# RWKV scan on the array's diagonal: 64x64x64 products in a parity-major layout, with ranks for its steps

## The chip, the cores and the metric

The kernel runs on one core of one Trainium2 chip. The metric is the device time of one execution in microseconds (us). The program is one launch; its engines are TensorE (PE; its weight loads are listed as PEld), VectorE (DVE), ScalarE (ACT), GpSimd (POOL) and SyncE (SP), and the DMA engines work from queues that an engine feeds. The trace's names with a q behind (SPq, ACTq) are what an engine's sequencer does itself, such as issuing a DMA.

## What is computed

One block of a diffusion transformer on 1024 tokens and 256 context tokens, width 1024, all in float32. The token mixer runs neighbourhood attention and a bidirectional RWKV-7 scan side by side, gates and merges them; an expert-choice mixture of experts follows.

```python
def rwkv_scan(r, decay, k, a, v, kk, S0, reverse, emit):
    def step(S, inp):
        r_t, w_t, k_t, a_t, v_t, kk_t = inp
        sa = jnp.einsum('bhvk,bhk->bhv', S, -kk_t)
        S = (S * w_t[:, :, None, :] + sa[..., None] * (kk_t * a_t)[:, :, None, :]
             + v_t[..., None] * k_t[:, :, None, :])
        y = jnp.einsum('bhvk,bhk->bhv', S, r_t) if emit else None
        return S, y
...
    for d in range(2):
        S_ctx, y_c = rwkv_scan(rc, *dirs_c[d], vrc, kkc, S0, d == 1, emit_ctx)
        _, y_l = rwkv_scan(r, *dirs[d], vr, kk, S_ctx, d == 1, True)
...
    y_rw = rwkv_readout(ys[0] + ys[1], r, v, [dirs[0][1], dirs[1][1]], g, p)
    out = (gate_na * (y_na @ p['w_pa']) + gate_rw * (y_rw @ p['w_pr'])) @ p['w_o']
```

There are 8 heads of 64 in the scan and 8 in the attention. `emit_ctx` is False here: the context is scanned only for its last state.

## The kernel before

**Stages.** Modulation and layer norms come first (to about 75 us). Then, to about 880 us, `proj` multiplies the tokens with slices of `w_in` (L258; each slice is loaded by SP's queue, split by ScalarE and GpSimd into a high and a low part, and multiplied in three passes), and for each of four pairs of heads `ct` and each direction `d` the function `feat` works out what the scan needs. It cuts the 1280 tokens into 20 chunks of 64 and takes them in five groups of four (`jb`), 40 groups in all. A group makes X (the scaled keys and receptances), BK (its partner), the masked products AQ of both, and BT (BK transposed on TensorE); SP's queue stores them to device memory as XD (L419), AQD (L430, L432), aD (L435) and BTD (L441). `inv` and `inv_off` make the 64x64 inverses of each chunk, WD; the last part of an inverse, `inv_off`, runs two passes of 32x32 products (L319), each copied by ScalarE (L320), and stores the result (L323).

**The scan** (`rwkv_chain`, L514 to L570) runs 20 step pairs, four over the context and sixteen "main" ones; a pair is one chunk in each direction, and the directions do not depend on each other. A step loads X, AQ, BT, its inverse WT (two DMAs, L533) and V (into the lower half of UV, L534), then
- L538: X times the state S, four products of 128x128 into RY; S holds each head's 64x64 on the diagonal of a 128x128 block, its other parts are zero;
- L541: the masked products times UV, added to RY; GpSimd has cleared the unused halves of AQ and UV (L529);
- L545, L546: R is minus the upper half of RY, the even heads copied by ScalarE, the odd ones by DVE;
- L550: the inverse times R, eight products of 64x64 that lie by turns in the upper left and the lower right quarter of the array;
- L553: the result copied to UV, half by DVE and half by ScalarE;
- L556: BT times UV, eight products; L561 and L562: DVE adds them to S and scales S by the decay, once for each half of the partitions;
- main steps only, L565 and L568: the masked products times UV once more, for the output Y, which ScalarE copies and whose store it issues from its own queue.

**What runs beside it.** After the features of the last pair 7 of the 16 slices of gates are left (`on_gate`, the same L258). Attention (`attention`, L572 to L660) runs 32 blocks, eight for each pair of heads. A block has score products (L588 to L591), maxima and scalings on DVE (L592 to L599), an exponential on ScalarE, and transposes and products with V (L606, L613). For each new pair of heads it loads K and Q in pieces (`qz`), rotates them on GpSimd and splits them on ScalarE and DVE. `readout` (L662) turns the outputs of the scan into the branch's features, `branch` (L699) multiplies either branch with its output weights, and `merge_top` and the experts follow.

**The order** is the framework's: it walks the program once and gives each engine its list of instructions, by priority; the priority is the place in the program, and `low_priority(tc,n)` puts what is in it n places back. The scan stands in the program ahead of the remaining gates and attention. A tile has one or two buffers; the queue of an engine is executed strictly in its order.

## Time and profile before

| | us |
|---|---|
| median of 3 runs | 3224.84 (3218.99 to 3229.81) |
| profiled execution, its own time | 3227.2 |
| span of its trace | 3225.4 |
| mean granted TensorE clock (share of full speed) | 0.953 |

Times below are us from the start of the span. In the tables by stretch "busy (x)" is the engine's busy time and its number of instructions, PEclk the clock that TensorE was granted, as a share of full speed, and DMA share the mean busy share of the 16 DMA engines. In the timeline a row is a run of alike instructions: its start, its length from the first start to the last end, and how many. An fp32 product leaves two records, each with its weight load.

### The profile page before, as it was taken

To read this page: it belongs to the slowest core of one execution; us is meant where nothing else is said; L and a number is where in the kernel's file an instruction comes from. 1 tells how busy PE (TensorE), PEld (TensorE's weight loads), DVE (VectorE), ACT (ScalarE), POOL (GpSimd) and SP (SyncE) were. 2 spreads that over 40 slices of the span, in tenths; PEclk is the share of its full clock that TensorE was granted. 3 is DMA by queue.
4 is the path that set the end of the run, shared out by engine and by line. 5 is a ranking of instruction groups with operands and counts; after the bars stand their busy time and mean duration, and the time that the engine had idled before them with its cause. 6 is when DMAs were issued, how large, how long until landed. Compare 5 with 4: busy or idle time off the path is not lost.

```text
span 3225.4 us, 47429 instructions
## 1 busy us (share of the span) xinstructions
PE 2975.9 (92%) x17900; PEld 2366.1 (73%) x17900; DVE 2361.4 (73%) x3207; ACT 1742.2 (54%) x2006; POOL 639.5 (20%) x511
## 2 busy tenths in 40 slices
PE   7999999997878978899879999999999999999995
PEld 4777776776667764477668888888888878888884
DVE  5245455544376769757788999888898888888887
ACT  5343343433234334322357777777777777777775
POOL 2233333333241227211000000111010111010004
PEclk8998999998889999899889999999999999999998
DMA  5245554555778766444589999999999999999985
GB/s 205 82 121 137 124 128 123 129 142 131 158 185 203 189 166 219 146 152 151 198 315 384 388 372 370 357 363 377 380 362 363 358 365 376 381 362 362 363 319 229
DMA packets 537641, 825.18 MB, mean 256 GB/s; under 512 B 206590, under 2 KB 335742, under 8 KB 537284
## 3 DMA queue, kind: packets, MB, share of 16 engines
q1 hardware_dynamic: 490876, 747.60, 67.5%
q10 hardware_dynamic: 41176, 55.01, 5.4%
q0 software_dynamic: 5360, 19.54, 2.3%
q8 instruction: 141, 2.31, 0.3%
q14 instruction: 88, 0.72, 0.1%
HBM read 732.49 MB, written 89.55 MB: 255 GB/s over the span
## 4 chain that ended last, share of the span: by engine, by line
PE 45%; DVE 8%; issue 4%; DMA 3%; ACT 2%; POOL 1%; ACTq 0%; POOLq 0%; DVEq 0%; SPq 0%
PE ph L1016 22%; PE ye L1031 14%; DVE lo L915 4%; PE po L752 3%; PE pA L709 2%; PE pt L1053 1%; DMA raw<-in_w_e_dram 1%; ACT hi L914 1%; DVE oh L856 0%; DVE dl L1055 0%; PE pl L828 0%; PE apt L606 0%; PE yp L613 0%; DVE s L599 0%; DMA wmod<-in_w_mod_dram 0%
## 5 line engine op out<-in xcount | busy, mean ns | idle before, releaser
L915 DVE TENSOR_TENSOR lo<-raw,hi 128x2048 fp32r<-128x2048 f32 (+1 forms) x560 | 1197.5, 2170 | 107.9 <-ACT hi L914 92.0
L914 ACT CAST hi<-raw 128x2048 fp32r<-128x2048 f32 (+1 forms) x560 | 1009.8, 1813 | 353.7 <-PE ph L1016 191.0
L1016 PE MATMUL ph<-lo,xh 128*128 128x512 f32 (+1 forms) x1536 | 456.7, 378 | 23.4 <-DVE lo L915 23.1
L1016 PE MATMUL ph<-hi,xh 128*128 128x512 f32 (+1 forms) x1536 | 448.9, 374 | 3.1 <-ACT xh L886 2.0
L1016 PE MATMUL ph<-hi,xl 128*128 128x512 f32 (+1 forms) x1536 | 448.2, 373 | 0.0
L1016 PEld LDWEIGHTS ph<-lo,xh 128*128 128x128 f32 x1536 | 267.6, 188 | 95.4 <-DVE lo L915 48.3
L1016 PEld LDWEIGHTS ph<-hi,xh 128*128 128x128 f32 x1536 | 271.5, 188 | 55.9 <-ACT xh L886 2.4
L1016 PEld LDWEIGHTS ph<-hi,xl 128*128 128x128 f32 x1536 | 270.8, 188 | 52.7
L258 PE MATMUL pp<-uh,whi 128*128 128x512 f32 (+1 forms) x832 | 266.2, 392 | 4.8 <-DVE th L334 3.1
L258 PE MATMUL pp<-ul,whi 128*128 128x512 f32 (+1 forms) x832 | 267.4, 392 | 0.0
L258 PE MATMUL pp<-uh,wlo 128*128 128x512 f32 (+1 forms) x832 | 261.8, 387 | 0.5 <-issue 0.3
L864 POOL DMA_INDIRECT gath<-table,idx x16 | 37.9, 2368 | 958.6 <-DVE oh L856 587.7
L1031 PE MATMUL ye<-lo,dh 128*128 128x512 f32 x704 | 222.5, 397 | 1.1 <-DVE lo L915 0.9
L1031 PE MATMUL ye<-hi,dh 128*128 128x512 f32 x704 | 219.7, 393 | 2.5 <-ACT hi L914 1.3
L1031 PE MATMUL ye<-hi,dl 128*128 128x512 f32 x704 | 218.9, 392 | 3.3 <-DVE dl L1055 3.3
L258 PEld LDWEIGHTS pp<-uh,whi 128*128 128x128 f32 x832 | 155.0, 195 | 42.2 <-issue 7.1
L258 PEld LDWEIGHTS pp<-uh,wlo 128*128 128x128 f32 x832 | 156.6, 196 | 38.2 <-issue 8.8
L258 PEld LDWEIGHTS pp<-ul,whi 128*128 128x128 f32 x832 | 156.3, 196 | 37.5 <-issue 10.0
L292 DVE TENSOR_TENSOR tmp<-AU,W 120x144 f32<-120x144 f32 (+24 forms) x248 | 93.0, 375 | 115.8 <-DMA WD<-AU 40.0
L1031 PEld LDWEIGHTS ye<-hi,dl 128*128 128x128 f32 x704 | 132.8, 189 | 32.1 <-DVE dl L1055 3.7
L207 POOL TENSOR_TENSOR wlo<-wraw,whi 128x512 fp32r<-128x512 f32 x86 | 113.6, 1341 | 211.4 <-ACT whi L206 141.0
L1031 PEld LDWEIGHTS ye<-hi,dh 128*128 128x128 f32 x704 | 131.1, 189 | 30.7 <-ACT hi L914 2.0
(334 smaller groups left out, 4488.8 us busy)
## 6 DMA issues: line engine op xcount, KB each, us to landing
raw<-in_w_e_dram SPq DMA_DIRECT2D x430, 1024.0 KB
raw<-in_w_e_dram SPq DMA_DIRECT2D x128, 768.0 KB
wraw<-in_w_in_dram SPq DMA_DIRECT2D x86, 256.0 KB
wmod<-in_w_mod_dram SPq DMA_DIRECT2D x48, 256.0 KB
BTD<-BT SPq DMA_DIRECT2D x40, 256.0 KB
cBT<-BTD SPq DMA_DIRECT2D x40, 256.0 KB
wmod<-in_w_mod_dram SPq DMA_DIRECT2D x16, 512.0 KB
XD<-X SPq DMA_DIRECT2D x32, 256.0 KB
```

The costliest lines, as they stand in the source:

```text
L207: nc.gpsimd.tensor_sub(l[:,ks],r,h[:,ks].bitcast(F32))
L258: nc.tensor.matmul(p,wt[:,k,:],ut[:,k,a:a+b],start=(k==0 and first),stop=(k==7 and last))
L292: nc.vector.tensor_tensor(v,AU[d][:,:,s,ts_][:,:,None,:].to_broadcast([120,2,nj,L]), W[d][:,:,js,s:s+1].to_broadcast([120,2,nj,L]),op=ALU. ...
L709: nc.tensor.matmul(pq[q],w[:,kk,:],y[:,kk,q*512:(q+1)*512],start=(kk==0 and first),stop=(kk==3 and last))
L752: nc.tensor.matmul(pq[q],a[:,r],w[:,q*512:(q+1)*512],start=(k==0 and first),stop=(k==7 and last))
L864: gi=nc.gpsimd.indirect_dma_start(out=g,out_offset=None,in_=table[:,:], in_offset=bass.IndirectOffsetOnAxis(ap=idx[:,:1],axis=0))
L914: nc.scalar.copy(hi[:,:2*w],r[:,:2*w])
L915: li=nc.vector.tensor_sub(lo[:,:2*w],r[:,:2*w],hi[:,:2*w].bitcast(F32))
L1016: nc.tensor.matmul(PH[m][j][:,:c.stop-c.start],x[:,k,:],y[:,c],start=(k==0 and a),stop=(k==7 and b))
L1031: nc.tensor.matmul(ye[j],l[:,k,:],rr[:,j*512:(j+1)*512],start=st and a,stop=sp and b)
L1053: for k in range(n): nc.tensor.transpose(pt[:,k,:],hd[:,(k0+k)*128:(k0+k+1)*128],ident)
```

## The change

**Layouts.** V, the outputs yD and the readout's operands are stored by the parity of the head: first the even heads, then the odd ones (`g_up`, `gn`, the rows of `w_pr` and `bonus` are permuted alike, the first three on the host). XD, BTD and WD have the pair of heads inside the chunk, so that one step's data of a tensor is one block; AQD is split into AVD (the products with V) and AUD (those with U), each with even heads on the upper and odd heads on the lower half of the partitions. `feat` therefore stores AQ in four DMAs a group (three before) and BT in four (one before); WT is loaded in one DMA (two before).

**The step.** V of all chunks is loaded once, by ten DMAs, and stays in SBUF. All products are 64x64x64, eight to a list, by turns in the two diagonal quarters of the array: 64 in a main step (before: 4 of 128x128, 16 of 128 rows by 64 columns and 16 of 64x64), 40 in a context step (before 4 and 8 and 16 of those). R and U are copied whole by ScalarE, S is added and scaled once on 128 partitions, and GpSimd clears nothing. Y is stored by two DMAs from SP's queue. Nothing is added or left out of what is computed.

**The ranks.** Step pair number s = 4j+n is issued at `low_priority(tc,2920-96*s)`, so that the first pair stands 2920 places back and each later one 96 places nearer.

```diff
@@ block(): tiles in device memory
-    XD=[dp.tile([4,128,20,128],F32,name=f"XD{d}") for d in range(2)]
-    AQD=[dp.tile([20,128,8,128],F32,name=f"AQD{d}") for d in range(2)]
-    BTD=[dp.tile([20,128,4,128],F32,name=f"BTD{d}") for d in range(2)]
-    WD=[dp.tile([4,40,64,64],F32,name=f"WD{d}") for d in range(2)]
+    XD=[dp.tile([20,128,4,128],F32,name=f"XD{d}") for d in range(2)]
+    AVD=[dp.tile([20,128,4,128],F32,name=f"AVD{d}") for d in range(2)]
+    AUD=[dp.tile([20,128,4,64],F32,name=f"AUD{d}") for d in range(2)]
+    BTD=[dp.tile([20,128,2,4,64],F32,name=f"BTD{d}") for d in range(2)]
+    WD=[dp.tile([20,2,64,4,64],F32,name=f"WD{d}") for d in range(2)]
@@ feat()
-                        if jb: nc.sync.dma_start(AQD[d][cs,64:128,2*ct:2*ct+2,:].rearrange("c p h f -> p c h f"),AQ[64:128])
                         for hh in range(2):
-                            if jb: nc.sync.dma_start(AQD[d][cs,0:64,2*ct+hh,64:128].rearrange("c p f -> p c f"),AQ[0:64,:,hh,64:128])
-                            else: nc.sync.dma_start(AQD[d][cs,64:128,2*ct+hh,:w].rearrange("c p f -> p c f"),AQ[64:128,:,hh,:w])
+                            nc.sync.dma_start(AVD[d][cs,hh*64:hh*64+64,ct,:w].rearrange("c p f -> p c f"),AQ[64:128,:,hh,:w])
+                            if jb: nc.sync.dma_start(AUD[d][cs,hh*64:hh*64+64,ct].rearrange("c p f -> p c f"),AQ[0:64,:,hh,64:128])
...
-                        nc.sync.dma_start(BTD[d][cs,:,ct,:].rearrange("c p f -> p c f"),BT)
+                        for j in range(2):
+                            for hh in range(2):
+                                nc.sync.dma_start(BTD[d][cs,hh*64:hh*64+64,j,ct].rearrange("c p f -> p c f"),BT[j*64:j*64+64,:,hh*64:hh*64+64])
@@ rwkv_chain()
+    VS={}
+    for b in (0,1,4,2,3):
+        VS[b]=p.tile([128,4,4,64],F32,name=f"V{b}",bufs=1)
+        for h,hh in zip(H,range(2)):
+            nc.sync.dma_start(VS[b][h],vD[b*256:b*256+256,hh].rearrange("(c p) a f -> p c a f",p=64))
+    def mm(o,l,r,first=None,stop=False):
+        for ct in range(4):
+            for hh,h in enumerate(H):
+                b=first is not None and len(first)<2
+                z=nc.tensor.matmul(o[h,ct],l[h,ct],r[h,ct],start=b,stop=stop,skip_group_check=True)
...
+        nc.sync.dma_start(WT,G["WD"][d][cc].rearrange("h s a t -> (h s) a t"))
...
+        mm(RU[:,0],AV[:,:,0:64],V,[],first)
+        if not first: mm(RU[:,0],X[:,:,0:64],S[d],stop=True)
+        R=p.tile([128,4,64],F32,name=f"R{d}",bufs=1)
+        nc.scalar.activation(R,RU[:,0],AF.Copy,scale=-1.0)
+        f=[]
+        mm(YS[:,1],BT[:,1],V,f)
+        if main:
+            mm(YS[:,0],AV[:,:,64:128],V,f)
+            mm(YS[:,0],X[:,:,64:128],S[d])
+        mm(RU[:,1],WT,R,stop=True)
+        nc.scalar.copy(U,RU[:,1])
+        mm(YS[:,1],BT[:,0],U,stop=True)
+        if not first: nc.vector.tensor_add(S[d],S[d],YS[:,1])
+        nc.vector.tensor_tensor(S[d],YS[:,1] if first else S[d],DL[d][:,:,cc:cc+1].to_broadcast([128,4,64]),op=ALU.mult)
+        if main:
+            mm(YS[:,0],AU,U,stop=True)
+            Y=p.tile([128,4,64],F32,name="Y",bufs=3)
+            nc.scalar.copy(Y,YS[:,0])
+            for h,hh in zip(H,range(2)): nc.sync.dma_start(yD[d][(cc-4)*64:(cc-3)*64,hh],Y[h])
     for j in range(5):
         for n in range(4):
-            for d in range(2): step(j,n,d)
+            with low_priority(tc,2920-96*(4*j+n)):
+                for d in range(2): step(j,n,d)
```

**DVE in the main steps.** In a row of DVE's list of the kernel before stand, among the maxima (L592, L593), scalings and copies of attention, the scan's R, S (addition and scaling, each twice) and UV:

```order
L546 TENSOR_SCALAR R0_8116<-RY0_8103 64x256
L561 TENSOR_TENSOR S1_7294<-S1_7294,US1_8055 64x4x64 x2
L562 TENSOR_TENSOR S1_7294<-S1_7294,DLs1_7298 64x4x64 x2
L617 TENSOR_TENSOR yl0_10230<-yp_10546,yh0_10229 128x4x32
L608 COPY pT_10609<-apt_10608 128x512
L593 ISA s_10646,m_10647<-sl_10656,bt_10639,m_10647 128x440
L593 ISA m_10647 128x1
L553 COPY UV0_8093<-US0_8119 64x4x64
L594 TENSOR_SCALAR m_10647<-m_10647 128x2
L546 TENSOR_SCALAR R1_8180<-RY1_8167 64x256
L561 TENSOR_TENSOR S0_7293<-S0_7293,US0_8119 64x4x64 x2
L562 TENSOR_TENSOR S0_7293<-S0_7293,DLs0_7297 64x4x64 x2
```

In the changed kernel the same part of the list holds S alone (L568, L569), among attention's L598 to L623:

```order
L600 TENSOR_SCALAR m_11375<-m_11375 128x2
L603 RECIPROCAL m_11375<-m_11375 128x2
L605 TENSOR_SCALAR s_11374<-s_11374,m_11375 128x696 x2
L568 TENSOR_TENSOR S1_7460<-S1_7460,YS1_8704 128x256
L569 TENSOR_TENSOR S1_7460<-S1_7460,DLs1_7462 128x256
L598 ISA s_11440,m_11441<-sc_11442,zero_11156 128x256
L598 ISA m_11441 128x1
L599 ISA s_11440,m_11441<-sl_11443,bt_11434,m_11441 128x320
L599 ISA m_11441 128x1
L568 TENSOR_TENSOR S0_7459<-S0_7459,YS0_8962 128x256
L569 TENSOR_TENSOR S0_7459<-S0_7459,DLs0_7461 128x256
L623 TENSOR_TENSOR yl0_11147<-yp_11332,yh0_11146 128x4x32
```

The copies of R and UV are gone from DVE, and the two state operations come once a step and not twice.

**TensorE where the last inverse ends and the scan begins.** In the kernel before, the second pass of the last inverse (L319) has gate products (L258) around it, and more of them stand between the first step's products:

```order
L319 MATMUL px<-AU_7184 32x32 x40
L258 MATMUL pp_10164<-uh,wlo 128x512
...
L541 MATMUL RY_7314<-UV_7305,cAQ_7302 64x64 x8
L541 MATMUL RY_7360<-UV_7351,cAQ_7348 64x64 x8
...
L258 MATMUL pp_10165<-uh,wlo 128x512
L550 MATMUL US_7326<-R_7323,cWT_7304 64x64
...
L550 MATMUL US_7326<-R_7323,cWT_7304 64x64 x7
L550 MATMUL US_7372<-R_7369,cWT_7350 64x64 x7
L556 MATMUL US_7326<-UV_7305,cBT_7303 64x64 x8
L556 MATMUL US_7372<-UV_7351,cBT_7349 64x64 x8
```

In the changed kernel the gates are L264, the inverse's products L325, and all the scan's products are the helper's L541:

```order
L264 MATMUL pp_10950<-uh,wlo 128x512
L325 MATMUL px<-AU_7350 32x32 x80
L541 MATMUL RU_7490<-V_7465,cAV_7481 64x64 x8
L541 MATMUL YS_7491<-V_7465,cBT_7485 64x64 x8
L541 MATMUL RU_7538<-V_7465,cAV_7529 64x64 x7
L541 MATMUL RU_7490<-R_7500,cWT_7483 64x64 x8
L541 MATMUL RU_7538<-V_7465,cAV_7529 64x64
L541 MATMUL YS_7539<-V_7465,cBT_7533 64x64 x8
L264 MATMUL pp_11015<-uh,whi 128x512
...
L541 MATMUL RU_7586<-V_7465,cAV_7577 64x64 x8
L541 MATMUL YS_7491<-U_7484,cBT_7485 64x64 x8
L541 MATMUL RU_7538<-R_7548,cWT_7531 64x64 x8
```

The inverse's two directions now stand together, the first steps' products come right behind them, and gates stand between the later products, 117 records of them behind the scan's first product (47 before). Of attention's 32 blocks 12 stand between the scan's first and last product (16 before). From the merge of the branches on, all five lists are the same in both kernels.

**SP's queue, one group of chunks in the features.** Before:

```order
L419 DMA XD_82<-X 128x512
L430 DMA AQD_84<-AQ 64x4x256
L432 DMA AQD_84<-AQ 64x4x64 x2
L435 DMA aD_90<-AQ 64x8x32 x2
L441 DMA BTD_86<-BT 128x4x128
```

And with the change:

```order
L426 DMA XD_82<-X 128x4x128
L438 DMA AVD_84<-AQ 64x4x128
L439 DMA AUD_86<-AQ 64x4x64
L438 DMA AVD_84<-AQ 64x4x128
L439 DMA AUD_86<-AQ 64x4x64
L441 DMA aD_92<-AQ 64x8x32 x2
L449 DMA BTD_88<-BT 64x4x64 x4
```

X's store has another layout in as many issues, the masked matrices' four issues replace three, and BT's four replace one.

## Rows read from the trace of the kernel before

**Rows 1.** The page, parts 1 and 5: engines over the span; gate and projection products.

```profile
PE 2975.9 (92%) x17900; PEld 2366.1 (73%) x17900; DVE 2361.4 (73%) x3207; ACT 1742.2 (54%) x2006; POOL 639.5 (20%) x511
...
L258 PE MATMUL pp<-uh,whi 128*128 128x512 f32 (+1 forms) x832 | 266.2, 392 | 4.8 <-DVE th L334 3.1
```

**Rows 2.** Busy time by stretch; columns in the first line.

```profile
core 0: us, PE busy (x) PEld busy (x) DVE busy (x) ACT busy (x) POOL busy (x), PEclk, DMA share, GB/s
100.00:780.00 680.00, 642.18 (x4106) 501.74 (x4104) 316.29 (x663) 254.60 (x424) 236.62 (x178) 0.95 0.49 124
...
880.00:960.00 80.00, 57.80 (x694) 49.01 (x692) 51.33 (x113) 23.96 (x55) 31.45 (x34) 0.85 0.68 175
...
1020.00:1080.00 60.00, 46.66 (x487) 38.41 (x489) 45.67 (x97) 23.14 (x56) 20.43 (x22) 0.80 0.70 177
1080.00:1160.00 80.00, 77.54 (x1069) 65.19 (x1063) 55.41 (x158) 34.22 (x82) 11.56 (x24) 1.00 0.82 204
1160.00:1220.00 60.00, 39.17 (x469) 33.81 (x468) 38.46 (x83) 18.69 (x45) 19.82 (x19) 0.86 0.63 162
1220.00:1300.00 80.00, 67.06 (x378) 34.73 (x378) 74.36 (x146) 35.70 (x77) 59.15 (x42) 0.91 0.64 200
...
1360.00:1420.00 60.00, 60.00 (x362) 46.83 (x361) 29.16 (x72) 16.37 (x37) 0.00 (x0) 1.00 0.41 132
```

**Rows 3.** Products of two scan lines: count, duration min/median/max (ns), first and last start.

```profile
L550 PE MATMUL US<-R,cWT x640: 218/218/366, 892.9 to 1208.5; 64*64 64x64 f32 x160
...
L565 PE MATMUL RY<-UV,cAQ x512: 219/222/368, 959.7 to 1211.7; 128*64 128x64 f32 x171
```

**Rows 4.** Timeline, TensorE's runs: start, duration, line, shape, count.

```profile
869.03 0.62 PE L258 MATMUL pp<-ul,whi 128*128 128x512 f32 x2
...
1085.37 0.68 PE L550 MATMUL US<-R,cWT 64*64 64x64 f32 x14
...
1092.27 1.16 PE L538 MATMUL RY<-S,cX 128*128 128x128 f32 x8
1093.36 1.15 PE L541 MATMUL RY<-UV,cAQ 128*64 128x64 f32 x16
```

**Rows 5.** TensorE by line, 1080 to 1160 us: count, busy us, mean ns.

```profile
L565 PE MATMUL RY<-UV,cAQ 128*64 128x64 f32 x190 | 15.3, 225 | 0.1
...
L588 PE MATMUL sc<-KH,Q 128*128 128x256 f32 x11 | 4.1, 370 | 0.0
```

**Rows 6.** DVE's scan lines, 840 to 1240 us: count, busy us, mean ns.

```profile
L562 DVE TENSOR_TENSOR S<-S,DLs 64x256 f32<-64x256 f32 x76 | 45.3, 596 | 2.2
...
L561 DVE TENSOR_TENSOR S<-S,US 64x256 f32<-64x256 f32 x76 | 31.7, 418 | 20.2 <-PE US L556 18.8
...
L546 DVE TENSOR_SCALAR R<-RY 64x256 f32<-64x256 f32 x40 | 16.6, 418 | 33.3 <-ACT R L545 32.6
L553 DVE COPY UV<-US 64x256 f32<-64x256 f32 x40 | 16.5, 414 | 6.9 <-PE US L550 4.4 <-issue 1.1 <-POOL UV L529 0.8
```

**Rows 7.** TensorE's waits, 100 to 780 us: total, times, longest.

```profile
PE pp L258 <- POOL wlo L207: 0.2, 1, 0.2
```

**Rows 8.** SP's issues of three stores: count, duration min/median/max (ns).

```profile
L430 SPq DMA_DIRECT2D AQD<-AQ x32: 574/580/707, 181.6 to 819.8; - x32
...
L432 SPq DMA_DIRECT2D AQD<-AQ x64: 581/698/2197, 182.3 to 821.1; - x64
...
L441 SPq DMA_DIRECT2D BTD<-BT x40: 359/565/1222, 175.4 to 814.9; - x40
```

**Rows 9.** Timeline at the scan's head: ScalarE, TensorE, SP's queue.

```profile
876.33 0.44 ACT L320 ACTIVATE AU<-px 128x320 f32<-128x320 f32 x1 [8.38 <-PE px L319]
...
880.98 0.89 PE L319 MATMUL px<-AU 32*32 32x32 f32 x80
...
882.38 1.82 SPq L323 DMA_DIRECT2D WD<-AU  x4
...
886.88 2.85 SPq L533 DMA_DIRECT2D cWT<-WD  x4
...
892.87 1.28 PE L550 MATMUL US<-R,cWT 64*64 64x64 f32 x32
```

**Rows 10.** The page, part 6: DMA issues, count and size of one.

```profile
BTD<-BT SPq DMA_DIRECT2D x40, 256.0 KB
```

92 lines of the change are left out of this document (31 added, 61 removed).

## The prediction

> **What bounds the kernel now.** I read the page first. Over the whole span TensorE is busy 92%, DVE 73% and ScalarE 54% [rows 1], but that average mixes stages, and the change reaches only the first 1420 us: from the merge of the two branches on, every engine's instructions stand in the same order in both kernels. So the table of stages comes next [rows 2]. From 100 to 780 us, where the projections run, TensorE is busy 642 of 680 us: a bound by products. From 880 to 1220 us, where the scan and attention share the engines, the picture alternates. From 1080 to 1160 us TensorE is busy 77.5 of 80 us, but in 880 to 960, 1020 to 1080 and 1160 to 1220 us it is busy only 57.8, 46.7 and 39.2 us, 56 us short of the 200, and the granted clock falls to 0.80 to 0.86. From 1220 to 1300 us DVE is the full engine (74.4 of 80), from 1360 to 1420 TensorE (60.0 of 60).
>
> The third view is when the scan runs. The products against the 64x64 inverse start at 892.9 us, and the products that only the main steps have run from 959.7 to 1211.7 us [rows 3]: 67 us for the four pairs of context steps and 252 us for sixteen pairs of main steps, 15.8 us a pair. In the good stretch 190 records of these products went by in 80 us [rows 5]; an fp32 product leaves two records, so a step leaves 16, and 11.9 steps in 80 us are 13.4 us a pair. In the same stretch 11 score products ran, two to an attention block, 5.5 blocks.
>
> The fourth view prices the products in the queue [rows 4]. A run lasts its starts plus one last duration (0.22 us, [rows 3]). So a record of the 128x128 products comes every (1.16-0.22)/7 = 0.134 us, one of the 128-row products into one half of the partitions every (1.15-0.22)/15 = 0.062, and one of the 64x64 products that alternate the two diagonal halves every (0.68-0.22)/13 = 0.035. Gate products (0.39 us alone, [rows 1]) come every 0.23.
>
> **The change part by part.**
>
> *The products of the scan.* A main step has now 4 products of 128x128, 16 of 128 rows into one half (the products by the masked matrices), 8 by the inverse and 8 for the state: 8x0.134+32x0.062+32x0.035 = 4.2 us of TensorE's queue. After it has 64 products of 64x64, 128x0.035 = 4.5 us. The halves alternate only within one product list; where the two directions' lists are laid into each other, a product follows one of its own half, and that is so for 380 of 2352 in the new order. For such a one I take the pace of the products that share a half: 2x(0.062-0.035) = 0.054 us, 17 us over the 32 main steps. Context steps go from 8x0.134+16x0.062+32x0.035 = 3.2 us to 80x0.035 = 2.8. So TensorE gets no relief: about +27 us in main steps (144+17 against 134). What the order says of one block of attention follows from the good stretch: 80-11.9x4.2 = 30 us for 5.5 blocks, 5.5 us each with all that switching costs.
>
> *DVE.* A step now costs DVE two additions and two scalings of the state on 64 partitions, half of R and half of UV: 31.7+45.3+16.6+16.5 = 110 us over the scan [rows 6]. After there is one addition and one scaling on 128 partitions, same free size, so the same duration each: about 38x0.42+40x0.60 = 40 us. ScalarE gets whole copies where it had halves, of equal free size, and a Y of 256 in place of 512 columns. GpSimd loses its memsets. So 70 us leave the engine behind which the scan's chain waits, and the chain meets DVE at one place a step, not at three (DVE's order, in the section on the change). That is no gain by itself: DVE is full only from 1220 to 1300 us. It is worth what it gives back of the 56 us that TensorE lacks.
>
> *Main steps.* By the new order 12 attention blocks stand between the scan's first and last step, 16 before. So after: 144+17+12x5.5 = 227 us of products. Before: 134+16x5.5 = 222 us, and it took 252: 30 us lost, mainly in two changes of the pair of heads (1020 to 1080 and 1160 to 1220 us). One such change is left inside the scan, with a lighter DVE: I take 8 us lost. 235 against 252: **-17**. Bounds: 0 (15.8 us a pair again) and -48 (no loss, blocks 2 us cheaper).
>
> *Context steps and gates.* The new order leaves 117 gate records behind the scan's first product, 47 before. Gates fill the scan's holes: 8x2.8+3+117x0.23 = 52 us, against 67: **-15**. Bounds 0 and -25 (gates all hidden).
>
> *The head of the scan.* The last inverse's second pass waits 4.2 us on TensorE behind gate products (ScalarE's copy of the first ends at 876.77, the pass runs at 880.98), then come stores, loads in halves and the first product at 892.87 [rows 9]. In the new order both passes stand side by side, and the loads are one DMA a step; new in front of them on SP's queue are 10 loads of V and 14 of the first steps. **-10**; bounds 0 and -16 (all 876.3 to 892.9).
>
> *Behind the scan.* Four blocks more are left, 22 us of queue. By the order three of them go among the branch products, where TensorE is full [rows 2]: **+17**. Bounds 0 (DVE-bound stretch with 13 us of free TensorE takes them) and +28.
>
> *Stores of the features.* Per group of chunks the transposed BK goes out in four issues in place of one, the masked matrices in four in place of three: 0.57 to 4x0.58 and about 0.5 more [rows 8], 2.2 us of SP's queue, 40 groups, 90 us. What is queued behind is the load of w_in; TensorE waited for its split only 0.2 us in 680 [rows 7], so most lies under products. In the last direction (780 to 840 us), where nothing covers, five groups are 11 us, half of it beside DVE's work: **+5**. Bounds 0 and +90. The yD stores move from ScalarE's queue to SP's and stand there in front of loads; these loads are two steps ahead (two buffers), 15 us, so I take 0, bound +10. V from SBUF drops a load per step.
>
> A rule of the Trainium skill speaks against these stores. In 100 to 780 us the DMA engines are busy 0.49 at 124 GB/s [rows 2], so full they would move 253 GB/s. The Trainium skill (DMA: Bandwidth & Descriptors, Specifications) asks for at least 512 B a transfer and says that smaller ones are read, modified and written. BT's rows fall from 512 to 256 B; by that rule, as an estimate, its 40 stores of 256 KB [rows 10], 10.5 MB, would take twice their 41 us, the share would be 0.55, still not the bound, and only the five uncovered groups would pay, 5 us more: -15 in place of -20 in the sum. No run here shows it yet; my sum goes by the rows.
>
> Sum: +5-10-15-17+17 = **-20 us** on the profiled execution's 3227.2 us (span 3225.4), 2.4 us above the median of 3224.84. I set it against the median: 3205 us.
>
> **The rivals.**
>
> *The holes close altogether.* For it: TensorE's waits there hang on DVE and ScalarE steps that are going. Against: the loads of K and Q and their DVE work for a new pair of heads stay. All 56 us and 4 us of the head: 3165.
>
> *TensorE's queue is the bound throughout.* For it: 77.5 of 80 us, and no fewer products. The main steps give nothing and the rest stays: 5-10-15+17 = -3, 3222, no change. That the change doesn't do what it says (halves don't overlap) ends here or worse: at 0.062 a record, 110 us more; the 0.035 of the inverse's products, which have the very shape, speaks against it.
>
> *SP's queue is the bound in the features.* Place: the feature stage. BT has one buffer, and its next copy on ScalarE waits until all four stores have been issued and landed; behind ScalarE queue the splits of w_in. Price up to 90 us; it decides from 30 of the 90 exposed on. At half, -25+45: 3245, slower. Against it: TensorE's 642 of 680 us.
>
> **How the numbers follow.** Forecast 0.40, holes close 0.22, queue-bound 0.18, SP's queue 0.20. A measurement of this kernel tells about 0.3% (10 us) from no change. Forecast (with a spread of some 15 us) and the first rival are faster, but for 0.06; the second is the same, but for 0.04: faster 0.58, same 0.20, slower 0.22. The range leaves out a tenth at each end: down to 3152, past the first rival, since the main steps' bound lies 31 us under what I took; up to 3242, near the slower rival. Faster cases alone span 3152 to 3215.
>
> **What would show it.** Right: DVE's two state operations 0.4 to 0.6 us each, about 40 us in all; main steps' products spread over some 235 us; runs of 64x64 records at 0.035; TensorE near full over the context steps; 100 to 780 us unchanged. Wrong: TensorE waiting for w_in's split before 780 us, or for BT (the slower rival); main pairs at 15.8 us with TensorE idle (holes not DVE's); records at 0.06 (halves not overlapping); more than 17 us added between the scan's last step and the merge.

## The result and the profile after

The changed kernel takes 3279.9 us (median of 4 runs, 3277.7 to 3280.4) against 3225.3 us: 1.0169 times as long, 95% interval 1.0152 to 1.0187. It is slower by 54.6 us, where 20 us less were forecast. Its profiled execution has a span of 3278.5 us, 53.1 us more.

The page's first part of the changed kernel, to be read beside [rows 1], busy time by engine:

```profile
PE 3018.6 (92%) x19868; PEld 2390.2 (73%) x19868; DVE 2291.9 (70%) x3049; ACT 1732.9 (53%) x2006; POOL 592.8 (18%) x429
```

DVE lost the 70 us that it was to lose (2361.4 to 2291.9), and TensorE got 42.7 us more. The table of stretches (columns as in [rows 2]):

```profile
100.00:780.00 680.00, 650.76 (x4108) 505.34 (x4108) 320.81 (x658) 256.10 (x424) 232.43 (x177) 0.95 0.51 124
...
880.00:960.00 80.00, 55.81 (x1008) 47.68 (x1008) 15.45 (x34) 18.94 (x42) 16.75 (x14) 0.84 0.63 184
960.00:1020.00 60.00, 51.30 (x1161) 45.55 (x1162) 26.88 (x63) 17.19 (x46) 11.55 (x9) 0.87 0.56 171
1020.00:1080.00 60.00, 58.00 (x1311) 49.63 (x1308) 18.44 (x55) 17.33 (x49) 0.00 (x0) 1.00 0.73 223
1080.00:1160.00 80.00, 72.39 (x1149) 55.96 (x1149) 34.81 (x88) 27.64 (x70) 10.06 (x8) 0.91 0.51 146
1160.00:1220.00 60.00, 53.19 (x854) 40.91 (x853) 26.96 (x87) 19.26 (x52) 6.62 (x6) 0.99 0.44 129
1220.00:1300.00 80.00, 65.88 (x301) 29.35 (x300) 60.79 (x119) 30.84 (x69) 60.19 (x44) 0.90 0.71 221
1300.00:1360.00 60.00, 52.42 (x326) 31.50 (x326) 52.67 (x126) 28.43 (x63) 26.07 (x23) 0.90 0.35 107
1360.00:1420.00 60.00, 45.93 (x257) 34.85 (x256) 37.72 (x91) 21.72 (x53) 8.30 (x6) 0.70 0.35 106
```

From 1020 to 1080 and from 1160 to 1220 us TensorE's holes of before are closed (58.0 and 53.2 us busy, 46.7 and 39.2 before). But DVE stands idle most of the time beside the scan (18.4 us busy of 60 from 1020 to 1080, 45.7 before), and behind it, from 1300 to 1420 us, TensorE lacks 22 us where it was nearly full. DVE's work beside the scan is attention's. The scan itself, by its lines (count, duration in ns, first and last start):

```profile
L541 PE MATMUL RU<-R,cWT x640: 218/218/366, 894.3 to 1203.4; 64*64 64x64 f32 x160
...
L541 PE MATMUL YS<-U,cAU x512: 218/218/365, 962.9 to 1208.4; 64*64 64x64 f32 x171
```

```profile
L568 DVE TENSOR_TENSOR S<-S,YS x38: 404/420/423, 917.1 to 1206.4; 128x256 f32<-128x256 f32 x38
```

Beside [rows 3]: the products by the inverses begin at 894.3 (892.9), those of the main steps' output run from 962.9 to 1208.4 (959.7 to 1211.7). So the scan ends 3 us earlier, and the kernel 53 us later. The loss lies behind the scan, and two places show it. A score product here is one of L588 (L594 in the changed kernel), of which a block has two. In the kernel before the 16th block of attention has its second one at 1146.50, and the first one of the third pair of heads stands right behind the scan's last products:

```profile
1210.95 0.98 PE L565 MATMUL RY<-UV,cAQ 128*64 128x64 f32 x14
1211.86 0.39 PE L588 MATMUL sc<-KH,Q 128*128 128x256 f32 x1
```

In the changed kernel the scan's last run of products begins at 1207.96; then come seven more score products of the second pair, the last at 1246.52, and the third pair begins only at 1282.36 (timeline, TensorE; between the last two stand the rest of the 16th block and products of the readout and of the modulation):

```profile
1207.96 0.68 PE L541 MATMUL YS<-U,cAU 64*64 64x64 f32 x16
```

```profile
1246.52 0.39 PE L594 MATMUL sc<-KH,Q 128*128 128x256 f32 x1
...
1282.36 0.38 PE L594 MATMUL sc<-KH,Q 128*128 128x256 f32 x1
```

The third pair of heads begins when both the scan and the first 16 blocks are done: its pool of tiles (`atq`) opens in the program behind those of the scan and of the first half of attention. It began 70.5 us later than before: 38 of the 74 us behind the scan's last product (1208.4) went by up to the 16th block's second score product, and 36 from that to the 17th block. From there to attention's last score product are 176.5 us (178.7 before), and from that to the first product of the merge 57.4 (75.5 before): 70.5 - 2.2 - 18.1 = 50.2 us, with which the merge begins (1516.3 after 1466.1).

### The profile page after: what moved, and what is told of

Its sections match the earlier page's. It is cut to its first block, busy times and chain, and to the rows that moved or that the text cites. A ratio compares the mean times of both kernels' runs of the same rounds, so it can differ in the third digit from the quotient of the medians.

```text
span 3278.5 us, 51242 instructions
## 1 busy us (share of the span) xinstructions
PE 3018.6 (92%) x19868; PEld 2390.2 (73%) x19868; DVE 2291.9 (70%) x3049; ACT 1732.9 (53%) x2006; POOL 592.8 (18%) x429
## 4 chain that ended last, share of the span: by engine, by line
PE 43%; DVE 6%; issue 3%; DMA 2%; ACT 2%; POOL 1%; ACTq 0%; POOLq 0%; DVEq 0%
PE ph L1023 21%; PE ye L1038 14%; DVE lo L922 4%; PE pA L716 3%; PE po L759 2%; DMA raw<-in_w_e_dram 1%; PE pt L1060 1%; ACT hi L921 1%; DVE oh L863 0%; DVE dl L1062 0%; PE pl L835 0%; PE yp L619 0%; ACT xh L893 0%; PE apt L612 0%; DMA acc<-yo,idx 0%
## 5 line engine op out<-in xcount | busy, mean ns | idle before, releaser
L264 PE MATMUL pp<-uh,whi 128*128 128x512 f32 (+1 forms) x832 | 268.4, 393 | 14.7 <-ACT gate L271 3.9
L264 PE MATMUL pp<-ul,whi 128*128 128x512 f32 (+1 forms) x832 | 269.0, 392 | 0.0
L264 PE MATMUL pp<-uh,wlo 128*128 128x512 f32 (+1 forms) x832 | 265.4, 389 | 0.2 <-POOL wlo L213 0.2
L264 PEld LDWEIGHTS pp<-uh,whi 128*128 128x128 f32 x832 | 155.3, 196 | 52.7 <-issue 7.1
L264 PEld LDWEIGHTS pp<-ul,whi 128*128 128x128 f32 x832 | 156.0, 195 | 40.8 <-issue 12.5
L264 PEld LDWEIGHTS pp<-uh,wlo 128*128 128x128 f32 x832 | 156.5, 196 | 35.5 <-issue 5.0
```

Source lines behind the costliest of these rows:

```text
L264: nc.tensor.matmul(p,wt[:,k,:],ut[:,k,a:a+b],start=(k==0 and first),stop=(k==7 and last))
```

## The experiments

Times are medians; the ratio is to the kernel before as it ran together with that version (medians 3222.9 to 3228.1). The columns of the table are read from TensorE's timeline and lines: the start of the first product by an inverse, of the scan's last product, of the second score product of the 16th block and the first of the 17th (the third pair of heads), of attention's last score product and of the merge's first product.

| kernel | inverse | scan's last | 16th block | 17th | last score | merge | time | ratio (95%) |
|---|---|---|---|---|---|---|---|---|
| before | 892.9 | 1211.7 | 1146.5 | 1211.9 | 1390.6 | 1466.1 | 3225.3 | |
| changed | 894.3 | 1208.4 | 1246.5 | 1282.4 | 1458.9 | 1516.3 | 3279.9 | 1.0169 (1.0152 to 1.0187) |
| e1 | 904.6 | 1107.5 | 1287.6 | 1310.0 | 1458.3 | 1515.1 | 3281.4 | 1.0177 (1.0151 to 1.0203) |
| e2 | 898.9 | 1230.7 | 1135.8 | 1230.8 | 1416.3 | 1476.4 | 3243.5 | 1.0059 (1.0043 to 1.0075) |
| e3 | 904.4 | 1252.0 | 1128.9 | 1252.1 | 1444.1 | 1504.3 | 3263.3 | 1.0113 (1.0089 to 1.0138) |
| e5 | 902.5 | 1209.8 | 1248.1 | 1283.7 | 1454.1 | 1515.9 | 3276.8 | 1.0159 (1.0133 to 1.0185) |
| e6 | 907.7 | 1278.8 | 1249.2 | 1278.9 | 1465.7 | 1528.8 | 3290.6 | 1.0200 (1.0183 to 1.0217) |
| e7 | 906.5 | 1228.1 | 1140.2 | 1228.2 | 1411.4 | 1491.4 | 3254.3 | 1.0091 (1.0074 to 1.0107) |
| e8 | 888.5 | 1136.1 | 1318.3 | 1340.5 | 1485.6 | 1543.1 | 3304.2 | 1.0239 (1.0222 to 1.0256) |
| e9 | 905.1 | 1209.7 | 1381.8 | 1404.1 | 1552.7 | 1609.3 | 3373.9 | 1.0467 (1.0443 to 1.0490) |
| e10 | 907.7 | 1151.9 | 1333.3 | 1355.8 | 1508.6 | 1565.5 | 3322.5 | 1.0297 (1.0269 to 1.0324) |
| e11 | 891.4 | 1191.5 | 1165.8 | 1198.3 | 1397.1 | 1454.1 | 3219.1 | 0.9981 (0.9970 to 0.9993) |
| e12 | 923.0 | 1268.3 | 1180.4 | 1268.5 | 1458.6 | 1519.8 | 3284.8 | 1.0185 (1.0162 to 1.0208) |
| e13 | 890.2 | 1208.4 | 1388.5 | 1410.8 | 1560.1 | 1616.6 | 3376.3 | 1.0475 (1.0446 to 1.0504) |

### The ranks taken away (e1), alone (e2), and all alike (e3)

```diff
@@ e1, in the changed kernel
-            with low_priority(tc,2920-96*(4*j+n)):
-                for d in range(2): step(j,n,d)
+            for d in range(2): step(j,n,d)
@@ e2, in the kernel before
-            for d in range(2): step(j,n,d)
+            with low_priority(tc,2920-96*(4*j+n)):
+                for d in range(2): step(j,n,d)
@@ e3, in the changed kernel
-            with low_priority(tc,2920-96*(4*j+n)):
+            with low_priority(tc,2920):
```

> The changed kernel with its ranks taken away: the scan's steps stand at their place in the program, everything else is as in the changed kernel. By the order 2 blocks of attention and 6 gate records stand between the scan's first and last product (12 to 13 blocks and 96 gate products in the changed kernel), 30 blocks behind it. Theory A (blocks left behind: what the scan gains in its stretch is lost by attention's blocks that are done later, and the ranks decide how many): scan alone at its products' 181.8 us plus some 30 us of waits, so it ends near 1110 us, and 30 blocks at the 11.2 to 12.8 us that a block took behind the scan in the two traces end at 1446 to 1494 us (1470 in the changed kernel): 3255 to 3305 us, that is, nothing or little gained by ending the scan 100 us earlier. Theory B (the features' stores are the cause): ranks play no part, 3270 to 3290 us. Theory C (the smaller products fill TensorE): scan alone as long as in the changed kernel, some 300 us, and 3350 us or more.

> The kernel before with the ranks of the change (2920-96s) and nothing else of it. By the order 16 blocks of attention stand inside the scan as before, no gate stands behind its first product, and 9 score records instead of 6 stand among the products of the branches. Theory A: same count of blocks inside, so within 10 us of the kernel before, 3215 to 3240 us. Rival (the ranks by themselves delay the scan's first steps behind 2920 places of gates and attention, and the end of attention hangs on the scan's end): slower by 30 to 50 us, 3255 to 3275. Theories B and C: no difference to the kernel before.

> The changed kernel with one rank for all steps, 2920, in place of 2920-96s. By the order 16 blocks of attention stand inside the scan (12 to 13 in the changed kernel, 16 in the kernel before) and 18 gate products behind the scan's first (96 and 17). Theory A: 3.5 blocks fewer behind the scan at 11.2 to 12.8 us each are 39 to 45 us less there, the scan longer by 3.5 times the 6.8 us that a block's products took beside it, 24, and shorter by 78 gate products at 0.25, 19 us: about 3280-42+24-19, 3235 to 3250 us. Theory B: nothing but the gates' 19 us, and these only if they fit ahead: 3260 to 3280. Theory C: 3270 to 3285.

Without ranks (e1) the scan runs almost alone and ends 100 us earlier than in the changed kernel, and attention ends at the same time: 1458.3 and 1458.9. That is theory A's lower half of its range: 30 blocks behind the scan took (1458.3-1107.5)/30 = 11.7 us each. Overlapping scan and attention as the change does it is worth nothing against running one after the other. Theory C, a scan alone of 300 us, falls (203 us from its first product by an inverse); B's range holds the time as A's does. The table also bears out in every kernel how the third pair starts: where the scan ends last (before, e2, e3, e6, e7, e12), the 17th block follows within 0.2 us of the scan's last products; where the 16th block ends last (changed, e1, e5, e8, e9, e10, e13), it follows 22 to 36 us after that block's score; in e11 it follows 6.8 us after the scan and 32 us after the 16th block's score, which fits the second kind.

One rank for all steps (e3) has all 16 blocks done by 1128.9, the scan then runs on by itself to 1252.0: 17 us better than the changed kernel, and 13 above theory A's 3235 to 3250; the time lies in B's range, for another reason than B's (e5 below). So the order is part of the loss, but not all of it. The ranks alone (e2) cost the old layout 19 us by the ratio, against theory A's ten: 20 main steps are done at the 16th block where 25 were, and the scan ends 19 us later. The rival had the sign right, and its 30 to 50 us were too many.

### Fewer issues for the stores (e5)

```diff
-                        for j in range(2):
-                            for hh in range(2):
-                                nc.sync.dma_start(BTD[d][cs,hh*64:hh*64+64,j,ct].rearrange("c p f -> p c f"),BT[j*64:j*64+64,:,hh*64:hh*64+64])
+                        for j in range(2):
+                            nc.sync.dma_start(BTD[d][cs].rearrange("c (h p) j a f -> p c h j a f",h=2)[:,:,:,j,ct],BT[j*64:j*64+64].rearrange("p c (h f) -> p c h f",h=2))
...
-                        for hh in range(2):
-                            nc.sync.dma_start(AVD[d][cs,hh*64:hh*64+64,ct,:w].rearrange("c p f -> p c f"),AQ[64:128,:,hh,:w])
-                            if jb: nc.sync.dma_start(AUD[d][cs,hh*64:hh*64+64,ct].rearrange("c p f -> p c f"),AQ[0:64,:,hh,64:128])
+                        nc.sync.dma_start(AVD[d][cs].rearrange("c (h p) a f -> p c h a f",h=2)[:,:,:,ct,:w],AQ[64:128,:,:,:w])
+                        if jb: nc.sync.dma_start(AUD[d][cs].rearrange("c (h p) a f -> p c h a f",h=2)[:,:,:,ct],AQ[0:64,:,:,64:128])
```

> The changed kernel with its ranks and its layout in device memory, but each group's masked matrices go out in two DMAs instead of four and BT in two instead of four (the two parities in one DMA, 64 partitions by 4 chunks by 2 by 64 or 128), so four issues as before the change. By the order 27 gate products stand behind the scan's first product instead of 96. Theory B: the first inverse product after the features moves back from 891.6 to about 881 us (881.6 before), the gates' 18 us return into the holes of the features, and 20 to 40 us of the 55 come back: 3240 to 3260 us. Theory A: the features' 10 us come back and some of the gates' time, the 12.5 blocks inside the scan stay: 3255 to 3272 us. Theory C: within 10 us of the changed kernel.

Three us come back of 55, less than the spread of e5's own runs (3273.9 to 3281.3): theory B falls here, and the forecast's slower rival with it. Theory A's 3255 to 3272 misses too; C's range holds the time. The stores do hold something up: in the changed kernel ScalarE waited 58.2 us for BT's buffer between 100 and 860 us, 10.8 before (waits of ScalarE: total, times, longest):

```profile
ACT BT L446 <- DMA BTD<-BT: 58.2, 20, 5.4
```

```profile
ACT BT L440 <- DMA BTD<-BT: 10.8, 7, 3.6
```

But only some 6 us of it reach DVE's loop over the inverses, which ends at 860.2 before, 870.3 changed and 864.1 in e5, and the rest of the head of the scan eats these (first product by an inverse at 902.5 in e5). The trace shows what went in there: of the 96 gate records that stood behind the scan's first product in the changed kernel 27 are left behind it, so 69 run ahead of the scan, and the context steps take 60.2 us in place of 68.6.

### Where the two ends meet (e6, e7), and the old scan alone (e8)

```diff
@@ e6, in e5
-            with low_priority(tc,2920-96*(4*j+n)):
+            with low_priority(tc,2920-78*(4*j+n)):
@@ e7, in e5
-            with low_priority(tc,2920-96*(4*j+n)):
+            with low_priority(tc,3200-66*(4*j+n)):
@@ e8, in the kernel before: the first score product of a block
-            nc.tensor.matmul(sc[:,hh],qt,KH[hh][:,T:TS],start=True,stop=False)
+            z=nc.tensor.matmul(sc[:,hh],qt,KH[hh][:,T:TS],start=True,stop=False)
+            tc.add_manual_dep(z.ins,G["last"].ins.name,mybir.DependencyInfo(mybir.DependencyClass.NoSync,mybir.DependencyReason.DATA),reason="order")
```

In e8 `G["last"]` is the scan's last product on TensorE, set in the main steps.

> The kernel with few store issues (e5) and a flatter row of ranks, 2920-78s in place of 2920-96s. By the order 29 of 32 main steps are done when the 16th block of attention begins, and all 16 blocks of the first two pairs of heads stand inside the scan (e5: all 32 done at the 16th, 12.5 blocks inside; the flat rank: 10 done; the kernel before: 25 done). Theory D, from the traces so far: the third pair of heads begins when the scan and the first 16 blocks are both done (before: its first score product at 1211.86, the scan's last product at 1210.95; changed: 1282.4, the 16th block's at 1246.5; flat rank 1252.1 and 1252.0; ranks alone 1230.8 and 1230.7), and from there attention takes another 175 to 192 us. So the two ends should meet: both at 1225 to 1250 us (182 us of scan products, 16 blocks at 6.4, 40 to 65 us of waits, from 902 us on), attention's end some 180 later, 3235 to 3262 us, and faster than e5 (3276.8). Theory E (in the new layout scan and attention get on badly in any order, the lists of small products being in each other's way): the joint stretch takes the 348 us of the flat rank or more, 3262 to 3280 us.

> As e6 with ranks 3200-66s: by the order no gate product behind the scan's first product, 5 main steps done at the fifth block, 13 at the ninth, 21 at the 13th and 27 at the 16th, the evenest mix of all (the kernel before 2, 13, 18 and 25). Theory D: the best mix, joint end at 1220 to 1245 us, 3230 to 3258 us. Theory E: no better than the flat rank, 3258 to 3275 us.

> The kernel before, in which attention's score products have an order wait behind the scan's last product on TensorE, so that the old scan runs without attention. It shows the old scan's own length; the new one alone took 147 us for its main steps (961.0 to 1107.8, ranks taken away). If the small products and the lighter DVE help the chain, the old main steps alone take 165 to 210 us (their products 4.2 us a step, 134 us, and DVE's three places a step); if not, 150 us or less. The whole: 32 blocks at 11.2 to 11.7 us behind the scan, so that attention ends 360 to 375 us after it: scan's end 1120 to 1170, attention's 1480 to 1545, 3290 to 3350 us. Theory D: slower than the kernel before by 60 us or more, since nothing runs beside the scan. A rival, that running beside each other gains nothing: within 20 us of the kernel before.

The two ends met in e6 as they should, at 1249 and 1279 us, and it is the slowest of the three: 3290.6. Theory D had the rule for the start of the third pair right, and its size for the joint stretch wrong: from the first product by an inverse to the 17th block e6 took 371 us where 323 to 348 were worked out. e7 took 322 us, as the kernel before (319), and 3254.3 us in all, inside D's range. The counts that its expectation gives for the order were wrong: 2, 9, 13 and 17 steps are done at its 5th, 9th, 13th and 16th block, an order like that of the flat rank and not the evenest. So the mix of e6 is bad, worse than theory E has it (3262 to 3280), and in e7 E falls (3258 to 3275): mixing early and then running the scan's rest alone is better in the new layout. e8 came out as expected in its main steps and its whole (187 us, 78 us slower than before): in the old layout the overlap is worth something.

The two scans alone (busy time by engine, main steps of e1 and of e8):

```profile
961.00:1108.00 147.00, 124.28 (x3935) 119.75 (x3933) 28.97 (x71) 35.41 (x94) 0.00 (x0) 1.00 0.76 227
```

```profile
949.00:1136.00 187.00, 140.03 (x2252) 127.54 (x2250) 78.28 (x187) 41.09 (x93) 27.55 (x56) 0.94 0.95 203
```

The new scan alone takes 147 us for its sixteen pairs, the old one 187, with DVE at 29 and 78 us. What the change set out to do it does, alone. The 40 us need not be DVE's alone: the same rows show the DMA engines 0.95 busy beside the old scan and 0.76 beside the new one, and a granted clock of 0.94 against 1.00, and in e8 TensorE waited for loads too (waits of TensorE, main steps of e8). No run here divides the 40 us between the layout's loads, the copies and the products.

```profile
PE RY L541 <- DMA UV<-vD: 9.7, 8, 3.0
```

Beside attention both layouts take the same 319 to 322 us at best. The question is then what the mix costs the new one.

### What a change of shape costs (e9, e10, e13)

A change of shape is counted here where a product follows one of another size on TensorE: its contraction rows and its output columns (64*64, 128*64 and so on), each rounded up to 32, 64 or 128. TensorE's timeline of the changed kernel has the places (start, length, line, shape, count). Sixteen 64x64 records in a row need (0.68-0.22)/15 = 0.031 us each. Laid between attention's products by twos, two of them and one transpose take 0.51 us, where 0.06 and 0.13 would do (a transpose in a run of four that lasts 0.66 us, (0.66-0.27)/3), which leaves 0.16 for each of the two changes:

```profile
1103.97 0.33 PE L541 MATMUL RU<-R,cWT 64*64 64x64 f32 x2
1104.23 0.33 PE L612 MATMUL apt<-ident,s 128*120 128x128 f32 x1
1104.48 0.32 PE L541 MATMUL RU<-R,cWT 64*64 64x64 f32 x2
1104.74 0.33 PE L612 MATMUL apt<-ident,s 128*120 128x128 f32 x1
...
1247.54 0.66 PE L612 MATMUL apt<-ident,s 128*128 128x128 f32 x4
```

In the kernel before, the masked products (128*64) lie between attention's products with V (120*64) without loss: the first three of these rows, four records, in 0.17 us:

```profile
1144.15 0.32 PE L613 MATMUL yp<-pT,vb 120*64 120x128 f32 x1
1144.20 0.28 PE L565 MATMUL RY<-UV,cAQ 128*64 128x64 f32 x2
1144.31 0.27 PE L613 MATMUL yp<-pT,vb 120*64 120x128 f32 x1
1144.32 0.22 PE L565 MATMUL RY<-UV,cAQ 128*64 128x64 f32 x1
```

The experiment puts products of another shape between the lists, which add zero to the sums, spread in e9, together in e10, and in e13 spread in the old layout.

```diff
@@ e9 and e10, in e1
+    Z=p.tile([128,128],F32,name="Z",bufs=1); nc.gpsimd.memset(Z,0.0)
+    def full(o,n):
+        for _ in range(n): nc.tensor.matmul(o[:,1],Z,Z[:,:64],start=False,stop=False,skip_group_check=True)
@@ e9: in mm(), with mid=1 in each of a main step's eight lists
+            if ct==1: full(o,mid)
@@ e10: behind one list of a main step
             mm(YS[:,0],AV[:,:,64:128],V,f)
+            full(YS[:,0],8)
@@ e13, in e8: behind every second product of L541 and of L565 in the main steps
+            if main and hd%2: full(RY[:,hd*64:(hd+1)*64])
...
+                if hd%2: full(RY[:,hd*64:(hd+1)*64])
```

> The change without ranks (e1, where the scan runs almost alone), and in each main step eight extra products of a zero 128x128 matrix with a zero 128x64 one, which add zero to the sums: one in the middle of each of its eight lists of 64x64 products. By the order TensorE changes 524 times between 64x64 products and products over all 128 rows while the scan runs (e1: 12; changed kernel 298; kernel before 122). Theory S (each such change costs TensorE some 0.17 us): in the trace of the changed kernel two 64x64 records take 0.06 us when 64x64 records follow, 0.25 when a product of attention follows, and records of attention take 0.2 us more when 64x64 ones follow; in the kernel before, products of 128 rows into half the partitions and those of attention follow each other at 0.05 without loss. So e9's scan takes 448 x 0.17 to 0.19, 76 to 85 us of TensorE more than e10's, of which the waits of the scan alone (23 us) can hide some: e9 slower than e10 by 55 to 85 us. Theory E' (the loss in the joint stretch is waits for other engines, not TensorE's changes of shape): e9 within 10 us of e10.

> As e9 with the same 256 extra products, but all eight of a main step behind one list: 76 changes between the two kinds by the order. 512 more records at 0.03 to 0.06 us and 64 changes at 0.17 to 0.19: the main steps, 147 us in e1, take 165 to 190 us, and the whole 3295 to 3325 us by theory S; by theory E' the same.

> The control to e9 in the old shapes: e8 (the kernel before with attention held behind the scan) with the same 256 extra products of a zero 128x128 matrix, eight in each main step, each standing by itself among the old products of 128 rows into half the partitions (L541 and L565); by the order TensorE changes 511 times between these and the extra ones. Theory S, in the form that only the products on 64 rows cost a change: 512 more records at 0.06 to 0.12 us, 30 to 61 us of products, of which the 50 us of waits of the old scan alone hide a part; main steps, 187 us in e8, take 190 to 225 us, that is 0 to 38 us more. Rival (any change of shape costs TensorE the 0.145 us that e9 and e10 showed for theirs): 511 x 0.145, 74 us, on top of the 30 to 61, less at most 50 hidden: main steps 241 to 272 us.

e9 is 51 us slower than e10 with the same products, a little less than the 55 to 85 of theory S; E' falls. e10 itself came out inside its range. The main steps of e9 run from 963.1 to 1209.7, 247 us, those of e10 from 967.6 to 1151.9, 184 us; TensorE's list changes its shape 499 times in the one and 69 times in the other, which makes 62/430 = 0.145 us a change. In both TensorE has next to no idle time in these steps, and the granted clock is 1.00, so the 62 us are time on TensorE and no wait for another engine (e9, then e10; columns as in [rows 2]):

```profile
963.10:1209.70 246.60, 246.60 (x4450) 212.44 (x4446) 28.95 (x71) 35.16 (x93) 0.00 (x0) 1.00 0.46 135
```

```profile
967.60:1151.90 184.30, 183.84 (x4447) 178.60 (x4443) 28.60 (x71) 35.21 (x93) 0.00 (x0) 1.00 0.60 181
```

The rows show where: two extra records take 0.37 us when 64x64 ones follow, and 0.23 by the run of sixteen in e10, (2.00-0.275)/15 each:

```profile
1041.48 0.43 PE L533 MATMUL YS<-Z 128*128 128x64 f32 x2
1041.85 0.45 PE L544 MATMUL YS<-V,cBT 64*64 64x64 f32 x8
...
1042.69 0.43 PE L533 MATMUL YS<-Z 128*128 128x64 f32 x2
1043.06 0.45 PE L544 MATMUL YS<-U,cAU 64*64 64x64 f32 x8
```

```profile
1044.56 2.00 PE L533 MATMUL YS<-Z 128*128 128x64 f32 x16
```

e13 shows that it is not only the products on 64 rows. In the old layout, too, the extra products of 128*128 cost each time they change places with those of 128*64: two in 0.36 us, and four of 128*64 in 0.38 where 4x0.062 = 0.25 would do. The main steps took 251 us against 187 in e8; theory S in its narrow form gave 190 to 225, the rival 241 to 272.

```profile
1040.10 0.45 PE L568 MATMUL RY<-UV,cAQ 128*64 128x64 f32 x4
1040.48 0.44 PE L521 MATMUL RY<-Z 128*128 128x64 f32 x2
1040.84 0.45 PE L568 MATMUL RY<-UV,cAQ 128*64 128x64 f32 x4
```

So each change of a product's shape costs TensorE some 0.12 to 0.16 us here, while 120*64 and 128*64 run mixed without loss in the kernel before. The Trainium skill states that changing the tiling mode drains TensorE (TensorEngine Tiling (Array Packing), Key Properties: "Mode switching requires drain"), and the runs agree, with 0.145 us as the price. Counted in the main steps' stretch of the timelines, the kernel before changes its shape 220 times, the changed one 298, e7 285, e6 347, e11 186; alone, the old scan 101 times and the new one 6. At 0.145 us the change costs 11 us net by that, and against its own scan alone, which hardly changes shape, 42. The old scan's 119 changes more in the mix are 17 us by the same price, so changes of shape account for some 25 of the 40 us that the new scan wins alone and loses in the mix; no run takes the other 15 apart.

### One piece of the change in the old shapes (e11), V from another queue (e12)

```diff
@@ e11, in the kernel before
-        nc.vector.tensor_scalar_mul(R[64:128],ry[:,:,1,:],-1.0)
+        nc.scalar.activation(R[64:128],ry[:,:,1,:],AF.Copy,scale=-1.0)
...
-            (nc.scalar.copy if hh else nc.vector.tensor_copy)(uv[:,:,hh,:],us[hh*64:hh*64+64])
+            nc.scalar.copy(uv[:,:,hh,:],us[hh*64:hh*64+64])
@@ e12, in e7
-            nc.sync.dma_start(VS[b][h],vD[b*256:b*256+256,hh].rearrange("(c p) a f -> p c a f",p=64))
+            nc.scalar.dma_start(VS[b][h],vD[b*256:b*256+256,hh].rearrange("(c p) a f -> p c a f",p=64))
```

> The kernel before with one piece of the change: the halves of R and UV that DVE copied are copied by ScalarE too (two instructions of 64 partitions each in place of one on each engine); products, layout and place in the program as before. By the order 16 blocks stand inside the scan and 29 of 32 main steps are done at the 16th (25 before). Theory F (what the scan lacked was DVE, and taking 33 us off it pays where the products keep their old shapes): the joint stretch of 319 us gets 10 to 20 us shorter, 3205 to 3217 us. Rival: ScalarE's two copies in a row cost the chain what DVE's one gave back, within 8 us of the kernel before, 3218 to 3234.

> e7 (few store issues, ranks 3200-66s) with the ten loads of V issued from ScalarE's queue instead of SP's. In e7 they stand on SP's queue from 836.0 to 843.8 in front of the stores of the last inverses, and the first product by an inverse runs at 906.5 (892.9 in the kernel before). Theory: the stores move up by up to 8 us, the inverse's last product from 893.3 to 885 to 888, and 4 to 8 us of the whole come back: 3246 to 3250 us. Rival: the loads of the first steps and ScalarE's own work are in the way all the same, 3252 to 3260.

e11 is the only version below the kernel before, and by little: 3219.1 us, 0.9981 of it (0.9970 to 0.9993). The time lies in the rival's range, 2 us above theory F's. Its joint stretch got shorter by 12 us up to the 17th block (307 us from the first inverse, 319 before), as F has it, and the merge begins 12 us earlier; five (of the medians) to ten (of the spans) of them reach the end. e12 went wrong by both of its theories: ten loads on ScalarE's queue took 18.66 us to issue (7.76 on SP's in e7), most of them waiting for an earlier DMA to land, and ScalarE did no work for 22 us (timeline of ScalarE and its queue):

```profile
835.32 18.66 ACTq L533 DMA_DIRECT2D V<-vD  x10
854.01 1.28 ACT L271 ACT_TABLE_LOAD   x1 [22.46 <-DMA V<-vD]
```

The gates that wait for ScalarE came later, and the first product by an inverse with them (923.0 against 906.5). Its joint stretch is longer than e7's too (345 and 322 us), which this does not explain.

## Why the prediction was wrong

**What bounds the kernel** held: the table of stretches was the view to go by, the features stayed bound by TensorE (650.8 of 680 us), and behind the merge's first product only 2.9 us were added.

**The products** held alone and failed in the mix. 64x64 records come at 0.031 us (0.035 in [rows 4]), a main step alone costs TensorE 121/32 = 3.8 us (4.5 forecast), and halves overlap. But a block of attention was priced at "5.5 us each with all that switching costs" from the old mix [rows 5], where scan and attention share the 128*64 shape. By the timeline from the first scan product to the last (886 to 1215 us in both), attention's transposes and products with V cost TensorE 0.12 to 0.18 us a record in place of 0.08 to 0.15, which with a block's 8 score records, 11 transposes and 22 products with V is 6.4 us a block in place of 5.1, and the scan's products in the main steps 154 us where alone they cost 121 (161 forecast, with 17 for products that follow one of their own half).

**DVE** held: the addition (L568) takes 0.42 us as forecast, the scaling (L569) 0.42 where 0.60 was taken, 38 each, 32 us in all where 40 were forecast, and the engine has 70 us less. What was not seen is that DVE would then stand idle beside the scan, since fewer blocks of attention were there: 107 us busy of 260 from 960 to 1220, 180 before.

**Main steps**: 245.5 us for 12.5 blocks, 235 forecast for 12, 252 before for 16. TensorE's holes closed in part, its idle time in the main steps falling from 35 to 18.5 us (30 to 8 forecast); the dearer mix took the gain.

**Context steps**: 68.6 us, 52 forecast, 67 before. The gate products that came in cost 24 us of TensorE, 27 forecast: the trace has 96 of their records behind the scan's first product and 17 before, where the order was read as 117 and 47. But they did not fill the holes: the last of them runs at 937.5, and from 937.9 to 962.9 TensorE is busy 11.2 us of 25.

**The head of the scan** held: from the end of DVE's loop over the inverses to the first product by one 24.0 us (870.3 to 894.3), 32.7 before; -8.7 of the -10.

**Stores of the features**: the loop ended 10 us later, +5 forecast. The slower rival, half of 90 us exposed, did not come about; e5 puts the issues' share at 3 us of the whole. By the estimate from the Trainium skill's rule on transfers under 512 B (DMA: Bandwidth & Descriptors, Specifications) the DMA engines' share from 100 to 780 us was to rise from 0.49 to 0.55; it rose to 0.51, and e5, which keeps the rows of 256 B, ends the loop within 4 us of the kernel before. No run here shows that rule to cost more than these 4 us.

**Behind the scan** is the step that failed: +17 forecast for four blocks, +53.5 measured from the scan's last product to the merge (254.4 before, 307.9 after). The count was nearly right (3.5 blocks more). The price was taken from TensorE's queue, 5.5 us a block, and was too low, and the place was wrong: the blocks left do not go "among the branch products, where TensorE is full", they stand in front of the third pair of heads, which begins when the scan and the first 16 blocks are both done. A block there takes nearer what attention takes by itself, 11.7 us (e1): 38 us for the 3.5 blocks up to the 16th block's second score product. And the change of heads, which lay beside the scan before, lies bare, another 36 us: together 74 us from the scan's last product (1208.4) to the 17th block (1282.4), 0.2 before, of which 18 were slack at the merge. e7, with all 16 blocks inside the scan, takes 263.3 us from the scan's last product to the merge. The [rows 2] of before had the sign of it: from 1220 to 1300 us DVE was full, 16 blocks in the 179 us behind the scan.

**The sum** on the span, measured against forecast: stores +10.1 (+5), head of the scan -8.7 (-10), context steps +1.8 (-15), main steps -6.5 (-17), behind the scan +53.5 (+17), and +2.9 behind the merge's first product (0): +53.1 in place of -20. Of the 73 us between them 36.5 are the step that failed, 17 the context steps and 10.5 the main steps.

**The rivals.** None was this mechanism. The one on the slower side had the sign by another cause. That TensorE's queue is the bound throughout was nearest to the truth for the main steps.

What is shown: the order decides (e1, e3, e5 to e7: from 3254 to 3291 us with one and the same step, and e2), when the third pair starts (read from all 14 traces, and tested only through the order), the price of a change of shape (e9, e10, e13), and that the new scan alone is 40 us shorter and in the mix not (e1, e7, e8). What stays open: why the mix of e6 is so slow. Its 62 changes of shape more than e7 make 9 of the 49 us between their joint stretches; TensorE's idle time in the main steps is 22 us more, in an order that is fixed ahead of the run, and its mean granted clock there 0.90 in place of 0.95; no run here took that apart. With e7, 13.6 us of its 29 lie ahead of the scan's first inverse product, and they were not won back.

## What to carry to other kernels

A stage that is shortened alone is worth what it leaves behind for the stages beside it: ask what starts when two things are both done, and price the work that is put behind by its pace there, not by its share of a queue. Ranks that hand one of two joined stages the engine only move the later end; in the new layout the better orders (e3, e7) ran the joined work early and the scan's rest alone. Where products of several kinds share TensorE, keep them in one shape or in long runs of each.

## What the runs showed of the hardware

- A change between product shapes (64*64, 128*64, 128*128) costs TensorE 0.12 to 0.16 us of fp32 work: 62 us for 430 of them, with TensorE never idle (e9 against e10). Products of 120*64 and 128*64 mix without loss.
- 64x64 fp32 records by turns in two diagonal quarters come every 0.031 us, and 16 pairs of scan steps alone kept TensorE busy 124 of 147 us at the granted clock of 1.00, its higher level.
- Ten DMA issues on ScalarE's queue, most of which waited for an earlier DMA to land, held that engine's work for 22 us (e12).
